# Decoder layer on one core: rotary tables held behind the last row tile of h, and one low part of w0 held behind the first tile's second half

## The chip, the core and the metric

The kernel runs on one core of a Trainium2 chip. The metric is the device time of one execution in microseconds (us), the median of several runs. TensorE is called PE here, VectorE DVE, ScalarE ACT, GpSimd POOL and the queue of SyncE, which issues most DMAs, SP.

## The reference, cut to what matters

One decoder layer on 512 positions of width 1024, in float32. The part in question is its start:

```python
mod = jnp.einsum("bd,de->be", jax.nn.silu(c), w_ada[l]) + b_ada[l]
shift1, scale1, gate1, shift2, scale2, gate2 = jnp.split(mod[:, None, :], N_MOD, axis=-1)
h = layer_norm(x) * (1.0 + scale1) + shift1
t = token_mixer(h, positions, w_in[l], b_in[l], ...)
...
proj = jnp.einsum("bsd,de->bse", h, w_in) + b_in
q, k, v, g_ret, c_val, c_gate, gate_a, gate_b = jnp.split(proj, IN_SPLITS, axis=-1)
...
inv_freq = ROPE_BASE ** (-jnp.arange(half, dtype=jnp.float32) / half)
ang = positions.astype(jnp.float32)[..., None] * inv_freq
cos = jnp.cos(ang)[:, :, None, :]
sin = jnp.sin(ang)[:, :, None, :]
```

The tables of cos and sin are used when q and k are rotated. The rest of the layer (convolution branch, retention, gates, output projection, gated MLP) is not touched.

## The kernel before, in words

**The start.** h is kept transposed, as eight row tiles of 128 channels by 512 positions, k = 0 to 7. For each k the loop over `ND` loads a piece `wa` of w_ada and a piece `w0` of w_in (128 rows, 768 columns: six units of 128 columns). DVE makes scale and shift of the tile by two dot products with `wa` (`dot`, L378; the addition at L444 completes `mods`). PE transposes the normalised x (L453, tile `xT`), ACT applies scale and shift (L454, tile `hf`), and the result is split in a high part (L456) and a low part (L457). `split_to` splits `w0` likewise: the high part `w0h` on ACT (L258), the low part `w0l` on DVE (L259). PE then adds three products for each of six units (L480, L481 with the low part of h, L484 with the low part of w0) into six PSUM banks, the tiles `u`, over all k. For k = 0 this is done in two halves of 256 positions; between them the third and fourth block of rows of x are normalised (`norm_x(2)`, `norm_x(3)`: statistics on DVE L245 to L254, one power on POOL L238, two scalings on ACT L393).

**The rotary tables.** `rotary_tables` is a chain on tiles of 128 x 256: some products on DVE, then rounds, in each of which ACT rounds a tile into `tr` (L419, L420) and DVE uses it. There is one tile `tr`, so a round begins when DVE has read the one before. Six rounds lead to the reduced angle; a seventh goes before the four ACT instructions that write the sine table `stab` (L438), an eighth before the four that write the cosine table `ctab`.

**What follows.** `values` makes v of the first two heads: four units of weights (`wh`, `wl`; split by `prefetch`, L146 on ACT and L147 on DVE, three buffers each, shared with `w0h` and `w0l`), each multiplied with four blocks of positions into four PSUM banks (L554 to L556, tiles `v`). PSUM has eight banks. Six hold the tiles `u`, so two blocks of v can begin at once; the third needs the bank that is read by `th` (ACT, L515), the fourth the bank read by `cv` (L517). After that the first rotations use the tables (`rotary`, L534).

**What sets the order.** The scheduler of the framework puts the instructions of each engine in a fixed order at build time, by the order in which the code issues them and by its own estimates; each engine then runs its list in that order and waits at an instruction until its operands and buffers are ready. `later(150)` makes the scheduler treat a block as if it stood 150 instructions later. `tc.issue_after(ins)` puts each instruction of a block that runs on the engine of `ins` behind `ins` on that engine; `done` is the DVE instruction of L457.

Of the kernel before, what the change touches and what calls it, by code (L numbers as in the profile page):

```python
# [9 lines left out]
F32 = mybir.dt.float32  # L10
F32R = mybir.dt.float32r
I32 = mybir.dt.int32
AF = mybir.ActivationFunctionType
ALU = mybir.AluOpType
# [6 lines left out]
ND = D // P  # L21
# [157 lines left out]
def block_kernel(ctx: ExitStack, tc: tile.TileContext, a, out):  # L179
    nc = tc.nc  # L180
    act = nc.scalar.activation
    tt = nc.vector.tensor_tensor
# [4 lines left out]
    @contextmanager  # L187
    def later(n):
        p = tc.cur_priority
        tc.cur_priority = p + n  # L190
        yield
        tc.cur_priority = p
# [23 lines left out]
    def vc(name, j=0, w=1):  # L216
        o, _ = VEC[name]
        return vec[:, o + j:o + j + w]
# [38 lines left out]
    def split_to(h, l, src, scale=None):  # L257
        act(h, src, AF.Copy)  # L258
        tt(l, src, h.bitcast(F32), ALU.subtract)  # L259
# [64 lines left out]
    def ft(tag, shape, dt=F32, bufs=1):  # L324
        uid[0] += 1
        return fp.tile(list(shape), dt, tag=tag, bufs=bufs, name=f"{tag}_{uid[0]}")
# [28 lines left out]
    def load_first(k):  # L355
        wa = ft("wa", [P, 2048], bufs=3)
        w = ft("w0", [P, 768], bufs=3)
        if k == 1:
            nc.sync.dma_start(w, a["w0"][k])
            nc.sync.dma_start(wa, a["wada"][k])  # L360
        else:
            nc.sync.dma_start(wa[:, :D], a["wada"][k][:, :D])
            nc.sync.dma_start(wa[:, D:], a["wada"][k][:, D:])
            nc.sync.dma_start(w, a["w0"][k])
        return wa, w
# [24 lines left out]
    def norm_x(s):  # L390
        rs, nb = layer_stats(xh[s])
        for j in range(2):
            act(xh[s][j], xh[s][j], AF.Identity, bias=nb, scale=rs)  # L393
# [14 lines left out]
    def rotary_tables():  # L408
        nc.vector.tensor_copy(A, posi)
        ts(A, A, cc("freq"), None, ALU.mult)  # L410
        nc.vector.tensor_copy(A1r, A)
        tt(A2, A, A1, ALU.subtract)
        c1, c2, c3, c4, c5 = C2PI
        ts(sm, A1, c5, None, ALU.mult)
        for src, c in ((A2, c4), (A1, c4), (A2, c3)):
            stt(sm, src, c, sm, ALU.mult, ALU.add)

        def rnd(dst, src, c=1.0):
            act(dst, src, AF.Identity, bias=cc("magic"), scale=c)  # L419
            act(dst, dst, AF.Identity, bias=cc("magic", 1))  # L420

        for src, c in ((A2, c2), (A1, c3), (A2, c1), (A1, c2), (A1, c1)):
            rnd(tr, src, c)
            stt(fr, src, c, tr, ALU.mult, ALU.subtract)
            if src is A1 and c == c1:
                rnd(tr, fr)
                tt(fr, fr, tr, ALU.subtract)
            tt(sm, sm, fr, ALU.add)
        for tab, shift in ((stab, 0.0), (ctab, 0.25)):
            if shift:  # L430
                ts(sm, sm, shift, None, ALU.add)
            rnd(tr, sm)
            tt(sm, sm, tr, ALU.subtract)
            ts(fr, sm, 0.49999994, -0.49999994, ALU.min, ALU.max)
            for half in range(2):
                for dst in range(2):
                    sgn = -1.0 if (dst == 0 and not shift) else 1.0
                    act(tab[64 * dst:64 * dst + 64, half * NT:(half + 1) * NT],  # L438
                        fr[64 * half:64 * half + 64], AF.Sin, scale=sgn * TWO_PI)

    def mod_pair(j, src):
        for t in range(2):
            dot(mods[:, 2 * j + t:2 * j + t + 1], src[:, t * D:(t + 1) * D])
        tt(mods[:, 2 * j:2 * j + 2], mods[:, 2 * j:2 * j + 2], bada[:, 2 * j:2 * j + 2], ALU.add)  # L444
# [4 lines left out]
    def first_h(k, hf, c):  # L449

        pt = ps("xT")
        for s in range(c.start // P, c.stop // P):
            nc.tensor.transpose(pt[:, s * P:(s + 1) * P], xh[s][k // 4][:, (k % 4) * P:(k % 4 + 1) * P], ident)  # L453
        act(hf[:, c], pt[:, c], AF.Identity, bias=mods[:, 2 * k + 1:2 * k + 2], scale=mods[:, 2 * k:2 * k + 1])  # L454
        hh, hl = h_h[:, k, c], h_l[:, k, c]
        (act(hh, hf[:, c], AF.Copy) if k else nc.vector.tensor_copy(hh, hf[:, c]))  # L456
        return tt(hl, hf[:, c], hh.bitcast(F32), ALU.subtract)  # L457

    for k in range(ND):
        if k + 2 < ND:  # L460
            lf.append(load_first(k + 2))
        if k == ND - 2:
            st.load(0)
        if k == ND - 1:
            st.load(1)
        wa, w0 = lf[k]
        mod_pair(k, wa)
        hf = ft("hf", [P, S], bufs=2)
        wh = base.tile([P, 768], F32R, tag="wh", bufs=3, name=f"w0h{k}")
        wl = base.tile([P, 768], F32R, tag="wl", bufs=3, name=f"w0l{k}")  # L470
        for n, c in enumerate((slice(0, 256), slice(256, 512)) if k == 0 else (slice(0, 512),)):
            if n:
                norm_x(2)
                norm_x(3)
            done = first_h(k, hf, c)
            if not n:
                split_to(wh, wl, w0)
            for u in range(6):
                w = slice(u * P, (u + 1) * P)
                mm(acc0[u][:, c], wh[:, w], h_h[:, k, c], start=(k == 0 and n == 0), stop=False, skip_group_check=True)  # L480
                mm(acc0[u][:, c], wh[:, w], h_l[:, k, c], start=False, stop=False, skip_group_check=True)  # L481
            for u in range(6):
                w = slice(u * P, (u + 1) * P)
                mm(acc0[u][:, c], wl[:, w], h_h[:, k, c], start=False, stop=(k == ND - 1), skip_group_check=True)  # L484
        if k == 0:
            with later(150), tc.issue_after(done.ins):
                rotary_tables()
            nc.gpsimd.tensor_scalar(bhalf, vc("bin", E_CV, 32), 0.5, None, ALU.mult)
# [39 lines left out]
    def rotary(i, pq, e, nm):  # L528
        sw = ht("sw", [P, S])
        b = vc("bin", e)  # L530
        act(sw[0:64], pq[64:128], AF.Identity, bias=b[64:128])
        act(sw[64:128], pq[0:64], AF.Identity, bias=b[0:64])
        f = ht("t1", [P, S], bufs=2)
        stt(f, pq, b, ctab, ALU.add, ALU.mult)  # L534
        tt(sw, sw, stab, ALU.mult)
        tt(f, f, sw, ALU.add)
        xh_ = ht(nm + "h", [P, S], F32R, bufs=2 if nm == "q" else 1)
        xl_ = ht(nm + "l", [P, S], F32R, bufs=2 if nm == "q" else 1)
        split_to(xh_, xl_, f)
        return f, xh_, xl_  # L540
# [150 lines left out]
    for i in range(NH):  # L691
        if i == 0:
# [3 lines left out]
            k = rotary(i, pk, E_K + i, "k")  # L696
            v2 = values(i)
        else:
# [14 lines left out]
            k = rotary(i, pk, E_K + i, "k")  # L713
# [149 lines left out]
    for j in range(ND):  # L863
        p_ = ps("yb")
        for half in range(2):
            wh, wl = st.get()
            for kk in range(8):
                k = 8 * half + kk
# [123 lines left out]
    for half in range(2):  # L992
        wh, wl = st.get()
# [195 lines left out]
    for n, R in enumerate((R1, R2, R2, R2, R1, R3)):  # L1189
# [3 lines left out]
        for q in range(6):  # L1193
# [16 lines left out]
            for kk in range(2 if q < 5 else 1):  # L1210
                k = 2 * q + kk
# [147 lines left out]
```

## Time and profile before

| | |
|---|---|
| median of 3 runs | 1053.08 us (1052.61 to 1053.3) |
| the profiled execution | 1051.99 us |
| its span, first to last instruction | 1050.2 us |
| mean granted PE clock | 0.997 of full |
| PE, DVE, ACT, POOL busy | 1025.7, 837.3, 494.5, 72.2 us |

The span is the part that the trace shows; 1.79 us of the profiled execution lie outside it. A busy time says how long an engine had work in hand, not whether it was late. An instruction's row in the timeline gives its start, its duration, and in brackets how long the engine was idle before it and what ended that.

### The profile page before, as it was taken

The numbers are of one execution on the slowest core, as the hardware profiler recorded it, in microseconds if no ns is written. First come the engines' busy times: TensorE is split into PE (matmuls) and PEld (weight loads), VectorE is DVE, ScalarE is ACT, GpSimd is POOL, SyncE is SP. The second block draws the span as 40 slices with busy tenths as digits, with TensorE's granted clock in tenths as the row PEclk, the third lists the DMA queues.
The fourth block names the chain that finished last, engine by engine and source line by source line (L and its number), as shares of the span: only waits on it lengthen the run. The fifth ranks groups of instructions, "written<-read, shape, count | busy, mean of one in ns | idle before, by whom it ended". The sixth has DMA issues, their size and how long they took to land.

```text
span 1050.2 us, 12939 instructions
## 1 busy us (share of the span) xinstructions
PE 1025.7 (98%) x4889; PEld 858.6 (82%) x4889; DVE 837.3 (80%) x1373; ACT 494.5 (47%) x766; POOL 72.2 (7%) x93
## 2 busy tenths in 40 slices
PE   5999999999999999999999999999999999999996
PEld 4778888888888888888888888899888888888785
DVE  7979999999789979789994445876666666669888
ACT  5675444443454354461353334264444444457661
POOL 1000302020211020000000000110000000000012
PEclk9999999999999999999999999999999999999998
DMA  9733745482749286368653246012223223245772
GB/s 343 280 107 137 193 146 124 165 190 88 190 154 198 93 252 153 120 227 296 235 224 120 81 165 255 21 41 89 113 81 108 94 87 115 81 155 186 252 218 91
DMA packets 57009, 164.50 MB, mean 157 GB/s; under 512 B 4337, under 2 KB 27121, under 8 KB 47218
## 3 DMA queue, kind: packets, MB, share of 16 engines
q1 hardware_dynamic: 43328, 139.11, 37.9%
q0 software_dynamic: 13328, 24.38, 10.9%
q8 instruction: 38, 0.62, 0.2%
q10 hardware_dynamic: 290, 0.18, 0.1%
q14 instruction: 25, 0.20, 0.1%
HBM read 161.56 MB, written 25.17 MB: 178 GB/s over the span
## 4 chain that ended last, share of the span: by engine, by line
PE 89%; DVE 4%; ACT 3%; DMA 2%; issue 1%; POOL 0%; SPq 0%; DVEq 0%; ACTq 0%; POOLq 0%
PE up L506 7%; PE up L507 7%; PE up L509 7%; PE yb L870 3%; PE gate L506 3%; PE gate L507 3%; PE yb L871 3%; PE yb L872 3%; PE gate L509 3%; PE v L554 3%; PE v L556 3%; PE v L555 3%; PE g L507 2%; PE g L506 2%; PE g L509 2%; PE o L644 2%
## 5 line engine op out<-in xcount | busy, mean ns | idle before, releaser
L147 DVE TENSOR_TENSOR wl<-stage,wh 128x1024 fp32r<-128x1024 f32 x177 | 212.5, 1202 | 100.9 <-PE up L509 57.4
L146 ACT ACTIVATE wh<-stage 128x1024 fp32r<-128x1024 f32 x177 | 184.7, 1044 | 219.5 <-PE up L507 56.1
L525 DVE SCALAR_TENSOR_TENSOR conv<-ci,vec,conv 128x512 f32<-128x512 f32 x240 | 176.8, 747 | 3.4
L506 PE MATMUL up<-h,wh 128*128 128x512 f32 x304 | 118.3, 389 | 0.0
L507 PE MATMUL up<-h,wh 128*128 128x512 f32 x304 | 118.3, 389 | 0.0
L509 PE MATMUL up<-h,wl 128*128 128x512 f32 x304 | 75.1, 389 | 0.0
L509 PEld LDWEIGHTS up<-h,wl 128*128 128x128 f32 x304 | 57.1, 188 | 11.9
L506 PEld LDWEIGHTS up<-h,wh 128*128 128x128 f32 x304 | 57.1, 188 | 11.8
L507 PEld LDWEIGHTS up<-h,wh 128*128 128x128 f32 x304 | 57.1, 188 | 11.8
L1169 PE MATMUL d<-wh,op 128*128 128x512 f32 x132 | 51.4, 391 | 0.7 <-DVE dtmp L1226 0.6
L1170 PE MATMUL d<-wh,op 128*128 128x512 f32 x132 | 51.4, 389 | 0.0
L1171 PE MATMUL d<-wl,op 128*128 128x512 f32 x132 | 51.2, 389 | 0.0
L554 PE MATMUL v<-wh,h 128*128 128x512 f32 x128 | 49.9, 390 | 0.9 <-ACT th L515 0.9
L870 PE MATMUL yb<-rh,wh 128*128 128x512 f32 x128 | 50.3, 393 | 0.0
L506 PE MATMUL gate<-h,wh 128*128 128x512 f32 x128 | 50.1, 392 | 0.0
L872 PE MATMUL yb<-rh,wl 128*128 128x512 f32 x128 | 49.9, 389 | 0.0
L507 PE MATMUL gate<-h,wh 128*128 128x512 f32 x128 | 49.8, 389 | 0.0
L555 PE MATMUL v<-wh,h 128*128 128x512 f32 x128 | 49.8, 389 | 0.0
L871 PE MATMUL yb<-rl,wh 128*128 128x512 f32 x128 | 49.8, 389 | 0.0
L556 PE MATMUL v<-wl,h 128*128 128x512 f32 x128 | 49.8, 389 | 0.0
L1060 ACT ACTIVATE u<-up,vec 128x512 f32<-128x512 f32 x44 | 34.3, 779 | 25.1 <-PE up L509 21.7
L507 PE MATMUL g<-h,wh 128*128 128x512 f32 x112 | 43.7, 390 | 0.0
(317 smaller groups left out, 2398.9 us busy)
## 6 DMA issues: line engine op xcount, KB each, us to landing
stage<-in_wup SPq DMA_DIRECT2D x22, 1024.0 KB, 4.8
stage<-in_wstep SPq DMA_DIRECT2D x21, 1024.0 KB, 4.8
wb<-in_wada SPq DMA_DIRECT2D x32, 512.0 KB, 5.6
stage<-in_wstep SPq DMA_DIRECT2D x16, 512.0 KB, 9.4
stage<-in_wret SPq DMA_DIRECT2D x8, 1024.0 KB, 5.2
stage<-in_wga SPq DMA_DIRECT2D x8, 1024.0 KB, 4.8
wa<-in_wada SPq DMA_DIRECT2D x14, 512.0 KB, 7.1
stage<-T SPq DMA_DIRECT2D x6, 1024.0 KB, 4.8
```

The costliest lines, as they stand in the source:

```text
L146: nc.scalar.activation(wh[:, :w], src, AF.Copy)
L147: nc.vector.tensor_tensor(wl[:, :w], src, wh[:, :w].bitcast(F32), ALU.subtract)
L506: mm(dst, wh[:, k * P:(k + 1) * P], hs[k][0], start=(k == 0), stop=False)
L507: mm(dst, wh[:, k * P:(k + 1) * P], hs[k][1], start=False, stop=False)
L509: mm(dst, wl[:, k * P:(k + 1) * P], hs[k][0], start=False, stop=(k == n - 1))
L525: stt(o, ci[:, t:t + S], vc("cw", i * CK + t), o, ALU.mult, ALU.add)
L554: mm(pv[s], h_h[:, k, sl], wh[:, r], start=(k == 0), stop=False)
L555: mm(pv[s], h_l[:, k, sl], wh[:, r], start=False, stop=False)
L556: mm(pv[s], h_h[:, k, sl], wl[:, r], start=False, stop=(k == ND - 1))
L870: mm(p_, wh[:, w], rs_[k][0], start=(k == 0), stop=False)
L871: mm(p_, wh[:, w], rs_[k][1], start=False, stop=False)
L872: mm(p_, wl[:, w], rs_[k][0], start=False, stop=(k == 15))
```

## The change

The tables are issued after the loop's last pass (k = 7) instead of its first, behind that pass's L457, and the low part of w0 of k = 1 is issued behind the L457 of the first tile's second half. The same instructions run on each engine; line numbers after the edit are 5 to 7 higher.

```diff
             done = first_h(k, hf, c)
             if not n:
-                split_to(wh, wl, w0)
+                if k == 1:
+                    act(wh, w0, AF.Copy)
+                    with tc.issue_after(first_tile.ins):
+                        tt(wl, w0, wh.bitcast(F32), ALU.subtract)
+                else:
+                    split_to(wh, wl, w0)
...
         if k == 0:
+            first_tile = done
+        if k == ND - 1:
             with later(150), tc.issue_after(done.ins):
                 rotary_tables()
             nc.gpsimd.tensor_scalar(bhalf, vc("bin", E_CV, 32), 0.5, None, ALU.mult)
```

How this moves the instructions is seen in the order of three engines. First DVE at the first tile's second half, before the change (`bnst`, `mv`, `ve`, `nb`: the statistics of x; `junk`: the dot products; `w0l_320` is the low part of w0 of k = 1):

```order
L254 SCALAR_TENSOR_TENSOR nb_218<-mv_212,rstd_216 128x1
L259 TENSOR_TENSOR w0l_320<-w_16_115,w0h_319 128x768
L247 BN_AGGR mv_225<-bnst_222 128x2
L249 TENSOR_SCALAR ve_227<-mv_225 128x1
L254 SCALAR_TENSOR_TENSOR nb_231<-mv_225,rstd_229 128x1
L378 SCALAR_TENSOR_TENSOR junk_313,mods<-wa_114,cb_94 128x1024
L378 SCALAR_TENSOR_TENSOR junk_315,mods<-wa_114,cb_94 128x1024
L456 CAST h_162<-hf_180 128x256
L444 TENSOR_TENSOR mods<-mods,bada 128x2
L457 TENSOR_TENSOR h_163<-hf_180,h_162 128x256
L409 CAST A_156<-pos_118 128x256
L410 TENSOR_SCALAR A_156<-A_156,cst 128x256
```

And the same place after it (here the low part is `w0l_271`):

```order
L254 SCALAR_TENSOR_TENSOR nb_218<-mv_212,rstd_216 128x1
L247 BN_AGGR mv_225<-bnst_222 128x2
L249 TENSOR_SCALAR ve_227<-mv_225 128x1
L254 SCALAR_TENSOR_TENSOR nb_231<-mv_225,rstd_229 128x1
L378 SCALAR_TENSOR_TENSOR junk_264,mods<-wa_114,cb_94 128x1024
L378 SCALAR_TENSOR_TENSOR junk_266,mods<-wa_114,cb_94 128x1024
L456 CAST h_162<-hf_180 128x256
L444 TENSOR_TENSOR mods<-mods,bada 128x2
L457 TENSOR_TENSOR h_163<-hf_180,h_162 128x256
L480 TENSOR_TENSOR w0l_271<-w_16_115,w0h_270 128x768
L378 SCALAR_TENSOR_TENSOR junk_305,mods<-wa_170,cb_94 128x1024
```

The low part has moved from before the statistics of the fourth block of x to behind L457, and the first instructions of the tables (`A`) are gone from here.

Second ACT where the loop ends and `values` begins, before the change (`wh_670` is the high part of the third unit of v):

```order
L146 ACTIVATE wh_662<-stage_513 128x1024
L146 ACTIVATE wh_666<-stage_513 128x1024
L419 ACTIVATE tr_160<-sm_159,cst 128x256
L420 ACTIVATE tr_160<-tr_160,cst 128x256
L146 ACTIVATE wh_670<-stage_552 128x1024
L438 ACTIVATE stab_155<-fr_161 64x256 x4
L419 ACTIVATE tr_160<-sm_159,cst 128x256
L420 ACTIVATE tr_160<-tr_160,cst 128x256
L438 ACTIVATE ctab_154<-fr_161 64x256 x4
L515 ACTIVATE th_595<-u_1_29_165,bhalf 128x512
L517 ACTIVATE cv_597<-u_0_28_164,bhalf 128x512
```

And after it, from the third unit on (left out are three more rounds of two instructions each):

```order
L146 ACTIVATE wh_670<-stage_503 128x1024
L419 ACTIVATE tr_160<-A_24_158,cst 128x256
L420 ACTIVATE tr_160<-tr_160,cst 128x256
...
L419 ACTIVATE tr_160<-sm_159,cst 128x256
L420 ACTIVATE tr_160<-tr_160,cst 128x256
L438 ACTIVATE stab_155<-fr_161 64x256 x4
L419 ACTIVATE tr_160<-sm_159,cst 128x256
L420 ACTIVATE tr_160<-tr_160,cst 128x256
L438 ACTIVATE ctab_154<-fr_161 64x256
L522 ACTIVATE th_595<-u_1_29_165,bhalf 128x512
L524 ACTIVATE cv_597<-u_0_28_164,bhalf 128x512
```

Before, one round stands between `wh_670` and `th`; now there are six (five ahead of `stab`, one behind it), and `th` stands behind the first of the four `ctab` instead of the last. On DVE the third unit's `wl_671` likewise stands ahead of all that follows the second round.

Third PE in `values`, before the change: the end of the second unit's products with the first two blocks, and the first product into the third block `v_660`, whose bank `th` frees:

```order
L554 MATMUL v_659<-wh_666,h_162 128x512
L555 MATMUL v_659<-wh_666,h_163 128x512
L556 MATMUL v_659<-wl_667,h_162 128x512
L554 MATMUL v_660<-wh_662,h_162 128x512
L555 MATMUL v_660<-wh_662,h_163 128x512
```

And after it:

```order
L562 MATMUL v_659<-wh_666,h_163 128x512
L563 MATMUL v_659<-wl_667,h_162 128x512
L561 MATMUL v_658<-wh_670,h_162 128x512
L562 MATMUL v_658<-wh_670,h_163 128x512
L563 MATMUL v_658<-wl_671,h_162 128x512
...
L562 MATMUL v_659<-wh_670,h_163 128x512
L563 MATMUL v_659<-wl_671,h_162 128x512
L561 MATMUL v_660<-wh_662,h_162 128x512
```

Before, 21 products of v stand ahead of the first that needs `th`; now 36 do, those of three units with the first two blocks.

## Rows read from the trace of the kernel before

**Rows 1.** The page, busy time of each engine over the span.

```profile
PE 1025.7 (98%) x4889; PEld 858.6 (82%) x4889; DVE 837.3 (80%) x1373; ACT 494.5 (47%) x766; POOL 72.2 (7%) x93
```

**Rows 2.** The timeline, first tile: start us, duration us, engine, line, instruction.

```profile
14.46 1.65 PE L480 MATMUL u<-h,w0h 128*128 128x256 f32 x6 [2.38 <-DVE h L456]
...
16.81 0.96 DVE L259 TENSOR_TENSOR w0l<-w,w0h 128x768 fp32r<-128x768 f32 x1
...
18.42 0.33 SPq L363 DMA_DIRECT2D wa<-in_wada  x1
18.47 0.96 PE L453 MATMUL xT<-cst,x 128*128 128x128 f32 x4
...
18.81 1.22 DVE L378 SCALAR_TENSOR_TENSOR junk<-wa,cb 128x1024 f32<-128x1024 f32 x1
...
21.22 0.29 DVE L456 CAST h<-hf 128x256 fp32r<-128x256 f32 x1
...
21.56 0.74 PE L480 MATMUL u<-h,w0h 128*128 128x256 f32 x4
...
23.82 0.86 PE L480 MATMUL u<-h,w0h 128*128 128x512 f32 x3
```

**Rows 3.** SP's own waits, first 70 us: waited for, us in total, times, longest.

```profile
SPq L363 <- DMA wa<-in_wada: 2.6, 1, 2.6
```

**Rows 4.** The timeline between k = 5 and k = 6.

```profile
46.58 1.03 PE L453 MATMUL xT<-cst,x 128*128 128x128 f32 x8
...
47.22 0.78 ACT L454 ACTIVATE hf<-xT,mods 128x512 f32<-128x512 f32 x1 [1.87 <-PE xT L453]
47.90 0.49 ACT L419 ACTIVATE tr<-A,cst 128x256 f32<-128x256 f32 x1
...
48.29 0.62 ACT L456 ACTIVATE h<-hf 128x512 fp32r<-128x512 f32 x1
...
48.96 1.21 PE L480 MATMUL u<-h,w0h 128*128 128x512 f32 x4 [1.35 <-ACT h L456]
```

**Rows 5.** The timeline from the loop's end into `values`.

```profile
56.14 1.06 ACT L146 ACTIVATE wh<-stage 128x1024 fp32r<-128x1024 f32 x1 [1.26 <-PE u L481]
57.10 1.68 ACT L438 ACTIVATE stab<-fr 64x256 f32<-64x256 f32 x4
57.30 0.39 PE L554 MATMUL v<-wh,h 128*128 128x512 f32 x1
...
57.55 1.23 DVE L147 TENSOR_TENSOR wl<-stage,wh 128x1024 fp32r<-128x1024 f32 x1 [1.14 <-PE u L484]
...
58.81 0.51 ACT L419 ACTIVATE tr<-sm,cst 128x256 f32<-128x256 f32 x1
...
59.35 0.51 ACT L420 ACTIVATE tr<-tr,cst 128x256 f32<-128x256 f32 x1
...
59.90 0.42 DVE L433 TENSOR_TENSOR sm<-sm,tr 128x256 f32<-128x256 f32 x1 [1.12 <-ACT tr L420]
...
60.35 0.29 DVE L434 TENSOR_SCALAR fr<-sm 128x256 f32<-128x256 f32 x1
...
60.68 1.70 ACT L438 ACTIVATE ctab<-fr 64x256 f32<-64x256 f32 x4 [0.82 <-DVE fr L434]
...
61.83 0.39 PE L556 MATMUL v<-wl,h 128*128 128x512 f32 x1
62.41 0.69 ACT L515 ACTIVATE th<-u,bhalf 128x512 f32<-128x512 f32 x1
...
63.15 0.50 PE L554 MATMUL v<-wh,h 128*128 128x512 f32 x1 [0.93 <-ACT th L515]
```

**Rows 6.** Stretches at the end: busy us of each engine, granted PE clock, DMA.

```profile
1040.00:1041.00 1.00, 0.27 (x3) 0.07 (x1) 1.00 (x2) 0.00 (x0) 0.93 (x1) 1.00 0.00 0
...
1042.00:1043.00 1.00, 0.00 (x0) 0.00 (x0) 1.00 (x3) 0.00 (x0) 0.00 (x0) 1.00 0.14 55
1043.00:1044.00 1.00, 0.00 (x0) 0.00 (x0) 0.97 (x3) 0.00 (x0) 0.00 (x0) 0.60 1.01 383
```

## Prediction

> **What bounds the kernel now.** I read the page first: PE is busy for 98% of the span [rows 1], so time is won or lost only where PE stands idle or runs slowly, and a wait of DVE or ACT counts only through PE. Then I read the timeline of the first 63 us, the only part that the change touches. Three places in it matter. In the first tile PE waits for the normalised second half: its products stop at 18.47 and go on at 21.56, behind the cast of h on DVE at 21.22 [rows 2]. Between k = 5 and k = 6 it transposes two tiles from 46.58 on and then waits 1.35 us for the high part of h on ACT [rows 4]. And in `values` it stops after the 21st product of v, which starts at 61.83, and goes on at 63.15, when `th` on ACT has read the PSUM bank that the third block needs [rows 5]. The reader is to see in the last one that `th` stands on ACT right behind the end of the rotary tables: `ctab` from 60.68, `th` at 62.41. So the tables already end on PE's path, by about 1.1 us.
>
> **The low part of w0, k = 1.** Before, it takes 0.96 us on DVE at 16.81 (its successor can start about 0.9 later), ahead of the last statistics of x [rows 2]. Behind L457 it leaves that chain. But the two dot products stand between the statistics and the cast, and the first of them needs `wa` of k = 1. SP waits for a load of `wa` until it issues L363 at 18.42 [rows 2, 3]; by order of issue that is the load for k = 1, so it landed then. The first dot product can move from 18.81 to 18.42, and cast and PE with it: 0.39 us gained. Bounds: 0, if the load landed later than I read, and 0.9, if it was there already. I take 0.39, because the cast waits for DVE's own line and not for ACT. The instruction itself now takes the place that the first table instructions leave, ahead of the dot products of k = 2; there it delays nothing, as PE needs it only in the third group of products of k = 1, some 3 us later.
>
> **The tables out of the loop.** Some 20 short DVE instructions and some ten of ACT leave k = 0 to 7. PE gets little for it: in the loop it waits for DVE almost nowhere. In the 1.35 us ahead of k = 6, ACT does `hf` at 47.22, a table instruction at 47.90 and h at 48.29 [rows 4]. The table instruction held h up by 0.39 us. In the new order its place is taken by `hf` of k = 7, a step like the one from 47.22 to 47.90, 0.68 us. So h of k = 6 comes 0.29 us later, not earlier. Bounds: 1.35 gained, if h were ready at once, and 0.29 lost; I take the loss, since the order says it. Net at the end of the loop: 0.39 - 0.29 = 0.10 us early, so `values` starts at 57.20 instead of 57.30.
>
> **The tables behind the loop.** Here the cost lies. On DVE the remaining rounds stand behind `wl_671`, the low part of v's third unit, and that waits for the last product of k = 7, which uses its buffer: 57.55 before [rows 5], 57.45 now. From there I walk the chain with the durations of rows 5, each step waiting for the one before.
> - `wl_671`, 1.23: 58.68. Then `fr` of the third round, at the 0.42 of a 128 x 256 operation and 0.04 to the next engine: 59.14. The rounding for it ran on ACT meanwhile.
> - Three rounds (c2, c1, and the rounding of `fr`). A round is two ACT instructions, 58.81 to 59.90, and one of DVE, 59.90 to 60.35: 1.09 + 0.45 = 1.54. Three are 4.62: 63.76.
> - One more addition on DVE, 0.45: 64.21. Round before the sine, 1.54: 65.75. Clamp on DVE (60.35 to 60.68), 0.33: 66.08.
> - Four `stab`, from 57.10 to the next ACT instruction at 58.81, 1.71: 67.79. Round before the cosine, 1.54: 69.33. Clamp, 0.33: 69.66.
> - One `ctab`, a quarter of 60.68 to 62.41, 0.43: 70.09. From `th` to PE, 62.41 to 63.15, 0.74: PE goes on at 70.83.
>
> PE has more to do until then: 36 products instead of 21. Their pitch is (61.83 - 57.30) / 20 = 0.2265 us, so they last 8.15 us, from 57.20 to 65.35. PE then stands for 5.48 us. Before, the 37th product of v started at 63.15 + 15 x 0.2265 = 66.55; now it starts at 70.83. Loss so far: 4.28 us. Nothing covers it: every product ahead of the fourth unit that needs no third bank is already among the 36. Behind `th` stand `cv`, three `ctab`, the first step of the convolution, `sw`, `sg` and then the fourth unit's high part; PE has 36 products, 8.2 us, for the two other blocks, and these ACT and DVE steps take about as long, so I count nothing more for them and up to 0.5 us in the range. On DVE some eight short instructions stand ahead of `wl_671`; they could push it by some 0.2 us, which is in the range too. No DMA moves: SP's list is the same, and the stages that it fills were asked for long before.
>
> **The clock.** Such a stop has a second price. At the end of the span PE's last product ends at 1040.27, and the granted clock, 1.00 until 1043, has a mean of 0.60 from 1043 to 1044 [rows 6]: as 0.5 is the lower of its two levels, 1.2 GHz against 2.4, it fell at about 1043.2, 2.9 us after the last product. A stop of 5.48 us is longer. What the lower level costs is seen at the start: 18 products of 256 columns take 4.01 us from 14.46 to 18.47, and the same 18 of the second half 2.26 us from 21.56 to 23.82 [rows 2]. That the first ran at the lower level is read from their pace alone. The loss is 1.75 us, if the clock comes back after as much work as there; it is 3.55 us if it came back only at 21.56 (half of the 7.1 us from 14.46), and 0 if the clock doesn't fall. I take 1.75, as products stand close together after this stop as they do in the first 18.
> The Trainium skill, "TensorE: Matmul & The Clock Gate", Part 1, calls the half clock the default, which sustained work lifts and idleness brings back, and says that the moment varies from run to run. The trace agrees on both sides of that, as above; by the rule the sum would be 4.28 where the clock happens to hold and 6.03 where it falls.
>
> **The sum.** 4.28 + 1.75 = 6.03 us. On the profiled execution: span 1050.2 + 6.0 = 1056.2, with the 1.79 outside it 1058.0. The median stands 1.09 above that execution, so 1059.1.
>
> **The rivals.**
> - *The clock holds.* The same stop, without the second price: 1053.08 + 4.28 = 1057.4. For it: one example of a fall, with a delay that need not repeat; the longest wait of PE inside the loop, 1.35 us, is no test. Against it: 5.48 is nearly twice 2.9. Chance 0.25.
> - *The stop is covered.* The chain runs faster than I walk it, or its waits overlap, so that the third block is free when PE comes to it or soon after. If PE goes on between 64.4 and 68.6, the time is within 2.1 us (0.2%, about what a measurement of this kernel can tell from no change) of 1053.08; I take 1053. For it: some of the steps are independent and durations overlap by some 0.1 us on one engine. Against it: the chain must be over 2 us shorter, and its rounds alternate between two engines with one `tr`. Chance 0.11.
> - *Faster.* The free DVE is worth more than the tail costs. If the chain ends before 65.35, the stop of 1.09 us (61.83 + 0.23 to 63.15) is gone; with the 1.35 us ahead of k = 6 and the net 0.10 that makes 2.54: 1050.5. It decides for faster once PE goes on before 66.45, which asks that a round cost some 0.7 us and not 1.54. Against it are rows 5, which show the round whole. Chance 0.05.
> - *More than the sum.* The stop is followed by a second, at the fourth unit of v, or the clock comes back late: 1061 to 1063. The slack of about half a microsecond there speaks for it, the slower PE in that stretch against it. Chance 0.06.
>
> **How the numbers follow.** The stop with the fall of the clock has 0.53 and gives 1059.1. The range takes in the clock that holds, less a larger gain at the first tile (0.9 for 0.39) and half of the wait ahead of k = 6: 1057.4 - 0.5 - 0.7 = 1056.2. Above it takes in the late return of the clock (1.8 more) and the small delays ahead of `wl_671` and at the fourth unit (0.6): 1061.5. That leaves out the covered stop, the gain, and a part of the last rival, about 2 in 10. Faster by over 0.2% has 0.05, within it 0.11, slower 0.84.
>
> **What would show it.** PE's products of the first tile's second half start about 0.4 us earlier. Between k = 5 and 6, `hf` stands twice on ACT ahead of h. In `values` PE starts 36 products without a break, is then idle for 5 to 6 us with ACT `th` as the releaser, and `th` starts near 70 us. The granted clock shows 0.5 for some microseconds around 70, and the products behind the stop have a pitch near 0.43 at first. If PE's idle time there is under 2 us, the walk along the chain is wrong; if it is there and the time is unchanged, my belief that PE's stops add to the end is wrong.

## The result and the profile after

The changed kernel takes 1058.2 us (median of 4 runs, 1057.39 to 1058.51); the kernel before 1052.84 (4 runs, 1050.41 to 1053.3; three of them are those given above). The ratio is 1.0054, its 95% interval 1.0042 to 1.0066: 4.4 to 6.9 us slower.

The page of the changed kernel: the span is 6.5 us longer, and PE has only 2.3 us more busy time than in [rows 1], for the same number of instructions. So PE was slower for a while, and the other 4.2 us it stood still.

```profile
span 1056.7 us, 12938 instructions
PE 1028.0 (97%) x4889; PEld 860.3 (81%) x4889; DVE 838.3 (79%) x1373; ACT 495.8 (47%) x766; POOL 71.7 (7%) x93
```

The list of PE's waits names the place (waited for, us in total, times, longest). The wait for `th` was 0.93 us before [rows 5] and is 5.5 now; the one for h of k = 6 was 1.35 [rows 4] and is 1.6.

```profile
PE v L561 <- ACT th L522: 5.5, 1, 5.5
PE u L485 <- ACT h L456: 1.6, 1, 1.6
```

The timeline of the first tile, after. The dot product starts as soon as `wa` has landed, and the second half's products follow at 20.68:

```profile
14.21 1.65 PE L485 MATMUL u<-h,w0h 128*128 128x256 f32 x6 [2.39 <-DVE h L456]
...
17.91 1.23 DVE L378 SCALAR_TENSOR_TENSOR junk<-wa,cb 128x1024 f32<-128x1024 f32 x1 [0.15 <-DMA wa<-in_wada]
...
20.33 0.29 DVE L456 CAST h<-hf 128x256 fp32r<-128x256 f32 x1
...
20.68 0.74 PE L485 MATMUL u<-h,w0h 128*128 128x256 f32 x4
```

From the first half's first product to the second half's it takes 6.47 us; before it took 21.56 - 14.46 = 7.10 [rows 2].

The timeline between k = 5 and k = 6, after: two `hf` in one row (x2), and only then the two h.

```profile
45.66 1.03 PE L453 MATMUL xT<-cst,x 128*128 128x128 f32 x8
...
46.30 1.45 ACT L454 ACTIVATE hf<-xT,mods 128x512 f32<-128x512 f32 x2 [5.97 <-PE xT L453]
...
47.64 1.15 ACT L456 ACTIVATE h<-hf 128x512 fp32r<-128x512 f32 x2
...
48.31 1.20 PE L485 MATMUL u<-h,w0h 128*128 128x512 f32 x4 [1.62 <-ACT h L456]
```

The timeline of `values` and of the unit behind it, after, three engines in order of time:

```profile
56.63 0.39 PE L561 MATMUL v<-wh,h 128*128 128x512 f32 x1
...
57.20 1.22 DVE L147 TENSOR_TENSOR wl<-stage,wh 128x1024 fp32r<-128x1024 f32 x1
...
58.79 0.51 ACT L419 ACTIVATE tr<-A,cst 128x256 f32<-128x256 f32 x1 [0.88 <-DVE fr L424]
...
60.34 0.51 ACT L419 ACTIVATE tr<-A,cst 128x256 f32<-128x256 f32 x1 [0.49 <-DVE fr L424]
...
61.88 0.51 ACT L419 ACTIVATE tr<-fr,cst 128x256 f32<-128x256 f32 x1 [0.49 <-DVE fr L424]
...
63.95 0.51 ACT L419 ACTIVATE tr<-sm,cst 128x256 f32<-128x256 f32 x1 [1.01 <-DVE sm L428]
...
64.56 0.39 PE L563 MATMUL v<-wl,h 128*128 128x512 f32 x1
...
65.81 1.69 ACT L438 ACTIVATE stab<-fr 64x256 f32<-64x256 f32 x4 [0.82 <-DVE fr L434]
...
69.72 0.67 ACT L522 ACTIVATE th<-u,bhalf 128x512 f32<-128x512 f32 x1
...
70.44 0.79 PE L561 MATMUL v<-wh,h 128*128 128x512 f32 x1 [5.49 <-ACT th L522]
71.03 0.63 PE L562 MATMUL v<-wh,h 128*128 128x512 f32 x1
...
75.72 0.61 PE L561 MATMUL v<-wh,h 128*128 128x512 f32 x1
76.15 0.42 PE L562 MATMUL v<-wh,h 128*128 128x512 f32 x1
...
86.87 0.39 PE L513 MATMUL cv<-h,wh 128*128 128x512 f32 x1
...
98.01 0.28 PE L606 MATMUL sc<-qh,kh 128*128 128x256 f32 x1
```

Three marks of the kernel before: the 37th product of v, the first product of the next unit (`cv`) and the first of the scores (`sc`):

```profile
66.68 0.39 PE L554 MATMUL v<-wh,h 128*128 128x512 f32 x1
...
80.28 0.39 PE L506 MATMUL cv<-h,wh 128*128 128x512 f32 x1
...
91.42 0.28 PE L599 MATMUL sc<-qh,kh 128*128 128x256 f32 x1
```

The last two come 6.59 us later after the change, and the span is 6.5 longer. So the whole loss has been made by the first product of `cv`, and nothing is won back behind it. It has two parts. The 37th product of v came at 66.68 and comes at 70.44: 3.76 us, the price of the wait. The other 2.83 are lost between there and `cv`, where PE has no further wait: its products stand 0.427 us apart (12 of them from 71.03 to 75.72, 4.69 / 11) instead of 0.2265. The windows of the changed kernel (busy us of PE, PEld, DVE, ACT, POOL, then the granted clock) show the lower level, 0.5 or 1.2 GHz, from within the stop (0.84 between 68 and 70, so from about 69.4) until shortly after 76:

```profile
66.00:68.00 2.00, 0.00 (x0) 0.00 (x0) 0.11 (x1) 1.94 (x5) 0.00 (x0) 1.00 0.00 0
68.00:70.00 2.00, 0.00 (x0) 0.00 (x0) 0.72 (x2) 1.15 (x4) 0.00 (x0) 0.84 0.00 0
70.00:72.00 2.00, 1.56 (x4) 1.27 (x5) 0.69 (x1) 1.95 (x5) 0.00 (x0) 0.50 0.00 0
...
76.00:80.00 4.00, 4.00 (x18) 3.23 (x18) 4.00 (x6) 3.46 (x5) 0.00 (x0) 0.98 0.19 29
```

### The profile page after: what moved, and what is told of

It reads as the page before. It is cut to its first block, busy times and chain, and to the rows that moved or that the text cites. A ratio compares the mean times of both kernels' runs of the same rounds, so it can differ in the third digit from the quotient of the medians.

```text
span 1056.7 us, 12938 instructions
## 1 busy us (share of the span) xinstructions
PE 1028.0 (97%) x4889; PEld 860.3 (81%) x4889; DVE 838.3 (79%) x1373; ACT 495.8 (47%) x766; POOL 71.7 (7%) x93
## 4 chain that ended last, share of the span: by engine, by line
PE 87%; DVE 6%; ACT 3%; DMA 2%; issue 1%; POOL 0%; SPq 0%; DVEq 0%; ACTq 0%; POOLq 0%
PE up L514 7%; PE up L513 7%; PE up L516 7%; PE yb L877 3%; PE gate L513 3%; PE gate L514 3%; PE yb L878 3%; PE yb L879 3%; PE gate L516 3%; PE v L561 3%; PE v L562 3%; PE v L563 3%; PE g L514 2%; PE g L513 2%; PE g L516 2%; PE o L651 2%
## 5 line engine op out<-in xcount | busy, mean ns | idle before, releaser
L561 PE MATMUL v<-wh,h 128*128 128x512 f32 x128 | 51.2, 400 | 5.5 <-ACT th L522 5.5
L562 PE MATMUL v<-wh,h 128*128 128x512 f32 x128 | 50.8, 397 | 0.0
```

The lines of the kernel that those rows point to most:

```text
L561: mm(pv[s], h_h[:, k, sl], wh[:, r], start=(k == 0), stop=False)
L562: mm(pv[s], h_l[:, k, sl], wh[:, r], start=False, stop=False)
```

## The experiments

The theory: `th` stands on ACT behind the chain of the tables, PE waits for the bank that `th` reads, and the stop costs twice, as waiting and as half clock. A rival: the time is lost to the busier DVE or to later tiles of h in the loop, and the stop at `th` only shows it. Another: the stop costs only its waiting. Line numbers shift by a few lines between the kernels. The kernel before ran beside them, 1052.65 us (21 runs) beside the first four and 1052.64 (20 runs) beside the last three. The diffs are against the changed kernel and show only what matters.

**The low part of w0 alone** (`e1_low_part_only`): the tables go back into the first pass.

```diff
         if k == 0:
             first_tile = done
-        if k == ND - 1:
             with later(150), tc.issue_after(done.ins):
                 rotary_tables()
```

> The tables stay in the loop's first pass; only the low part of w0 for k = 1 moves behind L457. The theory (the time is lost where th stands behind the tables on ACT) expects no stop of PE over 1.5 us in values, no fall of the granted clock there, and a small gain from the first tile, 0.4 to 0.9 us, so 1052.0 to 1052.4 against 1052.84. The rival that the moved low part itself costs time, by delaying the dot products of k = 2, expects 1053.5 or more.

Measured: 1052.01 us (11 runs, 1050.37 to 1052.91), ratio 0.9991, 0.9982 to 1.0. The wait for `th` is back at its old size:

```profile
PE v L560 <- ACT th L521: 1.0, 1, 1.0
```

Between the two halves of the first tile lie 20.51 - 14.19 = 6.32 us. So this part of the change brings about half a microsecond and is not what makes the kernel slower; its interval reaches from 1.9 us of gain to nothing.

**The tables alone** (`e2_tables_only`): the low part goes back.

```diff
-                if k == 1:
-                    act(wh, w0, AF.Copy)
-                    with tc.issue_after(first_tile.ins):
-                        tt(wl, w0, wh.bitcast(F32), ALU.subtract)
-                else:
-                    split_to(wh, wl, w0)
+                split_to(wh, wl, w0)
```

> Only the tables move behind the last pass; the low part of w0 stays where it was. The theory expects the whole loss, less the first tile's gain: PE idle 5 to 6 us ahead of the third block of v, the granted clock at 0.5 behind it, 1058.6 to 1059.3. The rival that the two edits need one another (the loss comes from their sum on DVE) expects under 1056.

Measured: 1058.91 us (5 runs, 1057.13 to 1060.7), ratio 1.0064, 1.0051 to 1.0078, inside the expected interval. The whole loss is the tables'. Its timeline shows a stop of the same length as the change's, to the hundredth; the clock came back earlier in this execution (the pitch is back to 0.23 behind the product at 74.26):

```profile
70.81 0.79 PE L556 MATMUL v<-wh,h 128*128 128x512 f32 x1 [5.49 <-ACT th L517]
...
73.96 0.46 PE L557 MATMUL v<-wh,h 128*128 128x512 f32 x1
74.26 0.39 PE L558 MATMUL v<-wl,h 128*128 128x512 f32 x1
```

This profiled execution is the fastest of the five, with a mean clock of 0.996; the other four show 0.993 or 0.994 and 1058.84 to 1060.7 us. The two halves of the first tile lie 21.03 - 13.93 = 7.10 us apart again, as before the change.

**`th` and `cv` ahead of the tables** (`e3_th_cv_first`): the tables stay behind the loop, but the two instructions that free the banks come first.

```diff
+    def gates(i, pcv, pcg):
+        th = pg("th")
+        act(th, pcg, AF.Tanh, bias=bhalf[:, 8 + i:9 + i], scale=0.5)
+        cv = pg("cv")
+        return th, cv, act(cv, pcv, AF.Identity, bias=bhalf[:, i:i + 1], scale=0.5)
...
         if k == ND - 1:
-            with later(150), tc.issue_after(done.ins):
-                rotary_tables()
             nc.gpsimd.tensor_scalar(bhalf, vc("bin", E_CV, 32), 0.5, None, ALU.mult)
+            *thcv, freed = gates(0, acc0[0], acc0[1])
+            with later(150), tc.issue_after(done.ins), tc.issue_after(freed.ins):
+                rotary_tables()
```

> Both edits as in the changed kernel, but th and cv of the first head are issued ahead of the tables and the tables behind cv on ACT. The theory expects the stop in values gone, the clock at 1.0, and with it also the 1.1 us that the kernel before lost there: 1051 to 1052. The rival that the loss is a backlog of late table work on DVE and ACT, which reaches PE wherever it stands, expects a stop later on (at the rotations or the fourth unit of v) and 1056 or more.

Measured: 1051.64 us (11 runs, 1050.63 to 1053.74), ratio 0.9992, 0.9983 to 1.0001. The tables stand behind the loop, PE waits 1.6 us ahead of k = 6 and starts v at 56.63 as in the changed kernel, yet the loss is gone: the first rival falls. What is left of the tables' place shows in PE's waits and in its products further on:

```profile
PE kT L596 <- DVE t L547: 0.8, 1, 0.8
PE cv L520 <- ACT sg L589: 0.6, 1, 0.6
...
91.42 0.28 PE L610 MATMUL sc<-qh,kh 128*128 128x256 f32 x1
```

The first product of `cv` starts at 79.13, 1.15 ahead of the kernel before. But the rotation now waits for tables that are ready only at 76, and at the first `sc` the kernel is exactly where the kernel before is. What PE wins by an unblocked bank, the late tables take back.

**Products of zero in the stop** (`e5_zero_products`): the wait stays, but PE has work in it. Eighteen products with an operand that is zero are added to the first two blocks of v, which adds nothing to them.

```diff
+    nc.vector.tensor_scalar(zero, ones, 0.0, None, ALU.mult)
...
+                if i == 0 and u == 2 and s == 1:
+                    for n in range(18):
+                        mm(pv[n % 2], zero, wh[:, (n // 2 % 2) * 512:(n // 2 % 2 + 1) * 512], start=False, stop=False)
```

> The changed kernel with 18 further products put behind the 36: they multiply a tile of zeros and add nothing to the first two blocks of v, and take PE some 4.1 us of the stop. th comes when it came, so PE can do nothing useful earlier. The theory that the stop has two prices, 3.9 us for the wait and 2.7 us for the half clock behind it, expects the granted clock to stay at 1.0 and 1055.3 to 1055.8. The rival that the half clock costs nothing, because ACT and DVE are late anyway at that place, expects 1058.2 as for the changed kernel.

Measured: 1056.04 us (5 runs, 1055.5 to 1057.24), ratio 1.0034, 1.0022 to 1.0047: 0.2 us above the expected interval, 2.2 below the changed kernel. Its timeline, and one of its windows, in which the granted clock is 1.00 as in all the others there:

```profile
64.84 4.35 PE L568 MATMUL v<-wh,zero 128*128 128x512 f32 x18
70.50 0.50 PE L563 MATMUL v<-wh,h 128*128 128x512 f32 x1 [1.31 <-ACT th L524]
```

```profile
70.00:72.00 2.00, 1.50 (x7) 1.24 (x8) 0.69 (x1) 1.95 (x5) 0.00 (x0) 1.00 0.00 0
```

PE goes on at 70.50, as late as in the changed kernel, and `cv` starts at 84.24: 3.96 us later than before, of which 70.50 - 66.68 = 3.82 is the wait. With no fall of the clock only 0.14 stands beside it. (The 3.9 and 2.7 us of the expectation were counted from 66.55; by the row at 66.68 they are 3.76 and 2.83.) The second rival falls as well: the clock is a price of its own.

**Two buffers for `tr`** (`e4_two_tr`): the rounds alternate between two tiles.

```diff
-    tr = ft("tr", [P, NT])
+    trs = [ft(f"tr{i}", [P, NT]) for i in range(2)]
...
+            dst = trs[tr_n[0] % 2]
+            tr_n[0] += 1
```

> The changed kernel with two tiles tr in turn, so that a rounding on ACT need not wait until DVE has read the one before. The theory (the length of the stop is the length of the chain of rounds) expects one round's wait less behind the third unit, th 1.5 us earlier at about 68.2, and a stop of about 4 us: 1056.7 where the clock still falls in it, 1054.1 where it doesn't. The rival that th waits for something other than the rounds (the third unit's split or the last product of k = 7) expects the stop at 5.5 us and 1058.2.

Measured: 1057.59 us (6 runs, 1057.22 to 1059.23), ratio 1.005, 1.0037 to 1.0063. The expectation was half met:

```profile
68.92 0.67 ACT L526 ACTIVATE th<-u,bhalf 128x512 f32<-128x512 f32 x1
```

`th` comes 0.8 us earlier and PE stands for 4.49 us instead of 5.49. But the rounds in `values` begin on ACT at 57.20, 59.13, 61.11 and 63.12, so 1.93, 1.98 and 2.01 us apart; in the changed kernel the five begin 1.93, 1.55, 1.54 and 2.07 apart. They did not close up, there is only one fewer of them behind the loop. So the run says that PE's stop follows `th`, not what a second buffer is worth. In the median the two kernels differ by 0.6 us, and their intervals overlap.

**`th` and `cv` between the sine and the cosine** (`e7_th_before_cosine`): the function is cut into the angle and the two tables, and the cosine is issued behind `cv`.

```diff
             with later(150), tc.issue_after(done.ins):
                 rotary_tables()
+                sine = table(stab, 0.0)
+            with tc.issue_after(sine.ins):
+                *thcv, freed = gates(0, acc0[0], acc0[1])
+            with later(150), tc.issue_after(freed.ins):
+                table(ctab, 0.25)
```

> The changed kernel with th and cv of the first head put on ACT between the four stab and the round of the cosine table. The theory expects th at about 67.5, a stop of 3.2 us, and 2.2 us less than the changed kernel: 1056.0 where the clock falls, 1053.4 where it doesn't; with a stop of this length either may be. The rival that a backlog of table work reaches PE anyway expects over 1057.

Measured: 1055.45 us (10 runs, 1053.12 to 1056.22), ratio 1.0023, 1.0013 to 1.0033. `th` begins at 67.88 and the stop is 3.34 us, close to what was expected; the clock fell, but only when PE was at work again, as the rows of its timeline and windows show:

```profile
68.62 0.51 PE L572 MATMUL v<-wh,h 128*128 128x512 f32 x1 [3.34 <-ACT th L464]
...
69.36 0.63 PE L574 MATMUL v<-wl,h 128*128 128x512 f32 x1
```

```profile
68.00:69.00 1.00, 0.38 (x2) 0.34 (x3) 0.00 (x0) 1.00 (x2) 0.00 (x0) 0.98 0.00 0
69.00:70.00 1.00, 1.00 (x4) 0.81 (x3) 0.69 (x1) 0.97 (x3) 0.00 (x0) 0.50 0.00 0
```

Seven of the ten runs lie between 1055.14 and 1056.22, with a mean granted clock of 0.994 to 0.996 each; three lie between 1053.12 and 1054.17, with 0.997 or 0.998, as much as the kernel before has in its profile. The run times lie around both expected values, as they would if the clock fell in the seven and hardly in the three. But only one of the ten has a trace, and the 20 runs of the kernel before vary as well, from 0.994 and 1055.11 us to 0.997 and 1050.92 us. So that it goes either way at a stop of this length is likely, not shown.

**The angle in the loop, the tables behind `cv`** (`e6_split`): the seemingly free DVE time of the loop is used for the six rounds of the angle, and only sine and cosine come behind the bank's release.

```diff
         if k == 0:
             first_tile = done
-        if k == ND - 1:
             with later(150), tc.issue_after(done.ins):
                 rotary_tables()
             nc.gpsimd.tensor_scalar(bhalf, vc("bin", E_CV, 32), 0.5, None, ALU.mult)
+        if k == ND - 1:
+            *thcv, freed = gates(0, acc0[0], acc0[1])
+            with tc.issue_after(freed.ins):
+                sine_tables()
```

> The angle of the tables stays in the loop as in the kernel before; only the sine and cosine part stands behind th and cv of the first head, and the low part of w0 for k = 1 behind L457. The theory expects no wait of PE for th, none later for the rotations, the clock at 1.0 and the kernel before less its 1.1 us stop and less 0.4 to 0.9 us at the first tile: 1050.7 to 1051.3 against 1052.7. A rival: the first rotations come late and PE waits for them, as it waited 1.4 us in all with all tables behind cv; then 1051.6 to 1052.2.

Measured: 1050.18 us (10 runs, 1049.34 to 1050.72), ratio 0.9974, 0.9965 to 0.9983, faster than both kernels: 1.8 to 3.7 us under the kernel before, and 0.5 us below the expected interval. In its timeline `th` runs at once behind the high part of v's third unit, and PE has no wait listed from 50 to 90 us:

```profile
56.26 0.67 ACT L463 ACTIVATE th<-u,bhalf 128x512 f32<-128x512 f32 x1
...
78.21 0.39 PE L524 MATMUL cv<-h,wh 128*128 128x512 f32 x1
...
89.34 0.28 PE L614 MATMUL sc<-qh,kh 128*128 128x256 f32 x1
```

`cv` and `sc` stand 2.07 and 2.08 us ahead of the kernel before. Unlike in `e3_th_cv_first` the tables are ready by 64.6, so nothing is given back.

## Why the prediction was right, point by point

**The stop in `values`: right, in place, cause and length.** PE did 36 products from 56.63 on and then stood for 5.49 us, with 5.48 forecast. That the two agree to 0.01 is chance: the forecast counts 36 products by their pitch, and counted like that the stop is 70.44 - 56.63 - 8.15 = 5.66. The rounds on ACT follow each other at 1.55 and 1.54 us, as walked; from the start of `wl_671` to PE's going on the walk gave 70.83 - 57.45 = 13.38 and the trace shows 70.44 - 57.20 = 13.24. The loss at the 37th product is 3.76 us against 4.28. Of the 0.52 between them, 0.13 is a slip in reading the kernel before: the walk put that product at 66.55 by the pitch, and the trace has it at 66.68, since the first products behind the short stop there come more slowly (63.15, 63.48, 63.72). The rest is that PE went on 0.39 earlier than forecast. The short DVE instructions ahead of `wl_671` did push it, to 0.57 us behind the first v product instead of 0.25.

**The first tile: right in kind, a little small.** I took 0.39 us. In the two kernels with the low part in its old place the halves lie 7.10 us apart, in the seven with it moved (the changed one and `e1`, `e3` to `e7`) 6.30 to 6.85: 0.25 to 0.80 gained. The bound was read rightly as well: in the changed kernel the dot product waits for `wa` itself. In that execution `wa` had landed at 17.91 and not at 18.42, and the second half started 0.88 early. Of these 0.88, 0.25 are no work of the change: the first half's first product already came at 14.21 instead of 14.46, and among all nine kernels it comes between 13.84 and 14.46.

**Between k = 5 and k = 6: right.** From the transposes to the products it takes 48.31 - 45.66 = 2.65 us after 2.38, so 0.27 lost where I took 0.29, and by the step named: `hf` of k = 7 ahead of h. With the 0.88 this makes `values` start 0.67 early (0.10 forecast).

**The clock: right that it falls, mis-sized.** I took 1.75 us from the pace of the first tile's first half; in the profiled execution of the changed kernel it was 2.83, since the clock came back 5.7 us after PE went on. The granted clock bears out the fall, but not the place that the 1.75 was taken from: in the kernel before it reads 1.00 there too, so half clock at the start rests on the pace alone, as the prediction says.

```profile
16.00:18.00 2.00, 2.00 (x11) 2.00 (x11) 1.91 (x7) 1.35 (x3) 0.55 (x1) 1.00 1.03 281
```

The table shows the two prices apart in each profiled execution. The first two columns are PE's stop and the delay of the 37th product against 66.68; the third is the delay of `cv` against 80.28; the fourth the difference of these two delays; the last how long PE worked at the lower level.

| kernel | stop | 37th product | `cv` | clock's part | at the lower level |
|---|---|---|---|---|---|
| changed | 5.49 | +3.76 | +6.59 | 2.83 | 70.44 to 76.15 |
| tables alone | 5.49 | +4.13 | +5.77 | 1.64 | 70.81 to 74.1 |
| two `tr` | 4.49 | +2.96 | +5.71 | 2.75 | 69.64 to 75.2 |
| `th` between the tables | 3.34 | +1.94 | +3.69 | 1.75 | 69.0 to 72.4 |
| zero products | 1.31 | +3.82 | +3.96 | 0.14 | never |

The clock's part is about half of the last column's length, as it must be at half pace: 5.71 / 2 = 2.86 in the changed kernel. It was 1.64 and 1.75 in two executions and 2.75 and 2.83 in two; the value I took is that of the cheaper pair, and 3.55 was a fair upper bound. The 0.14 without a fall of the clock is the slower start behind a stop, which the others have too. The runs without a trace point the same way: four of the five with the tables alone have the lower mean clock. But their times are 1.7 to 3.6 us above that of the one with the higher, more than the 1.1 to 1.2 between the two sizes, so something else varies too.

**The sum.** In the profiled execution 3.76 + 2.83 = 6.59 us against 6.03: the wait 0.52 smaller, the clock 1.08 larger. This execution, 1058.51 us, is the slowest of the four and has the lowest mean clock, 0.993; between the medians it is 5.36 us, so in the others, which have no trace, the clock may well have cost less. That the median of 1058.2 lies only 0.9 below the forecast of 1059.1 is in part luck, since the errors of the two terms have opposite signs. Of the 5.36, 0.24 come from a fourth run of the kernel before, 1050.41, which lowers its median from 1053.08 to 1052.84.

**The rivals.** That the clock holds is what `e5_zero_products` shows, 1056.04: that is 1.4 below the price I gave it. The covered stop asked that PE go on before 68.6, and it went on at 70.44. The gain did not come, since less DVE work in the loop brought PE nothing there: ahead of k = 6 it waits longer, not shorter. The prediction gave two bounds for "faster" that don't agree, PE going on before 66.45 and before 64.4; neither was reached. A second stop at the fourth unit, as in "more than the sum", did not show either.

## What to carry to other kernels

When a chain of small steps is moved out of a busy loop, look at what its engine does next for somebody else: here one 0.67 us ACT instruction that frees a PSUM bank stood behind some 12 us of table work, and that cost 5.4 us, while the same tables put behind it cost nothing that shows against the kernel before. Cut such a block by its users: the part that nobody is waiting behind goes into the slack, the rest behind the instruction that frees the bank, and then ask when its own users need it (`e3_th_cv_first` lost there what it won). A long stop of PE is to be priced with the clock, by half of the time that PE then works at the lower level: the four profiled stops of 3.34 to 5.49 us cost 1.64 to 2.83 us in this way, that of 1.31 us 0.14.

## What the runs showed of the hardware that was not expected

The granted clock does not fall at a fixed time after PE's last product. At the end of the span it fell 2.9 us behind it [rows 6]; in the stops it fell 3.25 us (two `tr`), 3.7 (`th` between the tables), 4.4 (changed kernel) and 5.3 (tables alone) behind the end of the last product ahead of the stop. With a stop of 3.34 us it fell 0.35 us after PE had gone on. So a wait that is over can still cost half pace afterwards, and two stops of the same 5.49 us cost 1.64 and 2.83 us behind them. The lower level lasted 6.8 us in the changed kernel (69.4 to 76.2) and with two `tr` (68.4 to 75.2), and 3.4 us with the tables alone (70.7 to 74.1) and with `th` between the tables (69.0 to 72.4); only what PE works in it is paid for. The Trainium skill, "TensorE: Matmul & The Clock Gate", Part 1, says that the moment at which the full clock comes, after matmuls have begun, differs between runs of one kernel. The returns here fit that, 3.3 and 5.7 us behind the same stop of 5.49 us, though in two kernels with one trace each; that the fall varies as well is what these rows add. What decides it in an execution was not settled here.
